# A decoder trunk on one core: the feed-forward output projection as seven half-size products

## The chip, the cores and the metric

The kernel runs on one core of a Trainium2 chip. The metric is the device time in microseconds (us) of one execution; the time before is the median of three runs. A core has TensorE (PE, matrix products, with its weight loads shown as PEld), VectorE (DVE), ScalarE (ACT), GpSimd (POOL) and SyncE (SP), each with an instruction queue of its own that is worked off in order, and 16 DMA engines that all queues share. SP, ACT and POOL issue transfers.

## The reference, cut to what matters

Two layers, each with a mixer (layer 0: forgetting attention beside a short convolution; layer 1: a gated linear recurrence), a cross-attention into 256 memory rows, and a feed-forward block; 512 positions, width 1024, all fp32. The change is in the feed-forward block's second product:

```python
D_MODEL = 1024; SEQ = 512; DEPTH = 2
D_FF = ((8 * D_MODEL // 3 + 255) // 256) * 256        # 2816

def rmsnorm(x, g):
    y = x * lax.rsqrt(jnp.mean(x * x, axis=-1, keepdims=True) + EPS)
    return y * g

def swiglu(h, w_gu, w_down):
    g, u = jnp.split(h @ w_gu, 2, axis=-1)
    return (jax.nn.silu(g) * u) @ w_down

    # in each layer, after the mixer and the cross-attention:
    h = rmsnorm(x, g_ffn_pre[layer])
    y = swiglu(h, w_ffn_gu[layer], w_ffn_down[layer])
    x = x + rmsnorm(y, g_ffn_post[layer])
```

## The kernel before

**Precision.** Every fp32 operand is split in two: a high part (an ACT cast to fp32r) and a low part (a DVE subtraction). A product is three matmuls: high x high, high x low, low x high (`mm3` L298, `OutProj.mm` L530). `split_out` (L506) does one split; for weights it has [128, 1024] elements.

**Order.** PE's order is written by hand in the whole kernel (`manual_schedule(engines={PE})`, L49). In the feed-forward stream ACT, DVE and POOL follow the program's order too (L868); elsewhere a scheduler orders them. SP is always ordered by the scheduler.

**Buffers.** `gpool` has 14 groups of [128, 4, 512]; `wst` four staging buffers for raw weights (tag `st`); `whi` and `wlo` four buffers each for their high and low parts; two PSUM pools, `bankA` and `bankB`, four banks of [128, 512] each.

**Stages of a layer.** Mixer, its output projection (`OutProj`, in two sweeps: `half0` for output columns 0 to 511, `half1` for 512 to 1023), memory projections (`memory_kv` L671), queries, scores and output projection of the cross-attention (`cross` L704), feed-forward (`ffn` L794). The feed-forward input product already runs as seven half-size products per chunk of 256 columns (`Winograd.stream` L443): 20 chunks, each of seven products of 12 matmuls with 256 columns, 84 in all; the first two column chunks are made before by `ws_gemm_split` (L354). Its activations y (22 k-tiles of 128 rows, 512 positions) go to DRAM by `put_y` (L806) and come back by `load_y` (L839), both on POOL's queue.

**The output projection before the change.** `pf` (L1272) is an `OutProj` with 22 k-tiles. `half0` (L563) loads the weights of two k-tiles at a time ([128, 2, 512], 512 KB), splits them, and multiplies them with all four tiles of 128 positions: 22 x 4 x 3 matmuls of 512 columns. `half1` (L570) does the same for the other columns, and leaves the last eight k-tiles (`TAIL`) for the end, one position tile after the other, so that the tail of one tile (`chain` L594: square sum, root, gain, residual; `next` L610: the next layer's pre-norm; `transpose` L617) lies beside the matmuls of the next tile. The root is `rstd` (L200): two small DVE operations and a power on POOL. In layer 0 the last two position tiles are transposed from `hook` (L620), which the next layer's `ws_gemm_split` calls between its first blocks of 24 matmuls; in layer 1 the rows go to the output.

Of the kernel before, what the change touches and what calls it, by code (L numbers as in the profile page):

```python
# [25 lines left out]
LEAD = 2  # L26
# [16 lines left out]
def trunk_kernel(ctx: ExitStack, tc: tile.TileContext, a: dict, out: bass.AP):  # L43
# [83 lines left out]
    def load_rows(w, k0, n, c0):  # L127
# [5 lines left out]
        return hi, lo  # L133

# [219 lines left out]
    def ws_gemm_split(w, c0s, hT, hook):  # L354

        wss = [w_chunk(w, c0) for c0 in c0s]
        banks = [[bankA() for _ in range(2)] for _ in c0s]
# [15 lines left out]
    class Winograd:  # L373
# [30 lines left out]
        def load(self, w, c0):  # L404
# [3 lines left out]
            for kh in range(2):  # L408
                nc.sync.dma_start(out=r[kh], in_=rows[:, 4 * kh:4 * kh + 4, c0:c0 + 256])
# [108 lines left out]
    class OutProj:  # L518
        def __init__(self, w, y, nk, g_post, g_pre, hT, first=bankA, second=bankB, final=False):
# [6 lines left out]
            self.ready = {}  # L526
            self.ahead = self.gate = None
# [10 lines left out]
        def half0_steps(self, ks, first, last):  # L538
# [5 lines left out]
            for n, k in enumerate(ks):  # L544
                wt = self.ready.pop(k) if k in self.ready else load_w(self.w, k, 2, 0, 512)
                if self.ahead:
                    for k2 in ks[n + LEAD:n + LEAD + 1]:
                        self.ahead(k2)
# [76 lines left out]

        def run(self):
            self.half0(range(0, self.nk, 2), True, True)
            self.half1()
# [165 lines left out]
    def ffn(layer, hT, prev, proj):  # L794
        w = a["w_ffn_gu"][layer]
        y = Feat([None] * NFF, [None] * NFF)

        y2 = dram.tile([P, NFF, 512], F32, name=f"y2_{layer}")
        yraw, yback = {}, {}

        def y_rows(jp):

            yraw[jp] = wst.tile([P, 2, 512], F32, tag="st", name="yr")
            return yraw[jp]

        def put_y(jp):  # L806
            nc.gpsimd.dma_start(out=y2[:, 2 * jp:2 * jp + 2, :], in_=yraw[jp])

        def act(jp, s, ub):
            y_ = y_rows(jp)  # L810
            for m in range(2):
                nc.vector.tensor_tensor(out=y_[:, m, :], in0=s[m], in1=ub[m], op=ALU.mult)
            put_y(jp)

        def chunks(jp):
# [10 lines left out]
            def up(m, sl, ps, sb, op):  # L826
                if not y_:
                    y_.append(y_rows(jp))
                ym = y_[0][:, m, :]
                nc.vector.tensor_tensor(out=ym[:, sl], in0=ps, in1=sb, op=op)  # L830
                mult = lambda: nc.vector.tensor_tensor(out=ym, in0=ym, in1=s[m], op=ALU.mult)
                if m == 1:
                    mult()
                    put_y(jp)
# [4 lines left out]
        def load_y(i):  # L839
            n = min(4, NFF - 4 * i)  # L840
            yback[i] = f(group("yb"))
            nc.gpsimd.dma_start(out=yback[i][:, 0:n, :], in_=y2[:, 4 * i:4 * i + n, :])

        def parts(jp):
            if jp // 2 not in yback:
                load_y(jp // 2)
            yg = group("y")
            split_out(yback[jp // 2][:, jp % 2 * 2:jp % 2 * 2 + 2, :], yg[:, 0:2, :], yg[:, 2:4, :])
            for m in range(2):
                y.hi[2 * jp + m], y.lo[2 * jp + m] = yg[:, m, :], yg[:, 2 + m, :]  # L850

        def side(left):

            if left == 3:
                load_y(0)
            if left:
                return {}
            raw = [load_raw(proj.w, k, 2, 0, 512) for k in (0, 2)]
            for i in (1, 2):
                load_y(i)  # L860

            def weights(n):
                proj.ready[2 * n] = split_w(raw[n], 2, 512)

            return {"a": lambda: weights(0), "b": lambda: parts(0), "c": lambda: weights(1), "d": lambda: parts(1)}

        gb, ub = ws_gemm_split(w, [0, FF], hT, prev.hook)
# [5 lines left out]
        proj.y = y  # L873
# [426 lines left out]
```

## Time and profile before

| | us |
|---|---|
| median of three runs (lowest, highest) | 1419.03 (1418.71, 1419.05) |
| the profiled execution | 1419.26 |
| its span, first to last instruction | 1417.5 |
| layer 0's output projection of the feed-forward | 622.6 to 744.1 |
| layer 1's | 1291.2 to 1411.0 |

Times of single steps are read from the profiled execution, counted from the start of its span; that execution lasted 1.8 us longer than its span. A row of a group ("lines") gives line, engine, operation, tiles and shapes, count, busy time and mean duration, and the idle time before it with what ended it. A row of the timeline gives start, duration, engine, line, operation. A row of windows gives, for a stretch, the busy time of PE, PEld, DVE, ACT and POOL (instructions), the granted clock of PE as a share of full speed, the share of the 16 DMA engines, and GB/s. A row of DMA issues ends with the median time from issue to landing. PE's instructions overlap, so the distance between their starts, not their duration, is what one costs.

### The profile page before, as it was taken

The page shows a single profiled execution, that of the slowest core. Times are in us where ns is not written, and L with a number is a line of the kernel's source. Part 1 is how long each engine was busy: PE and PEld are TensorE (multiplying, and loading weights), DVE is VectorE, ACT ScalarE, POOL GpSimd, SP SyncE. Part 2 cuts the span into 40 slices and gives each one's busy share as a digit, 9 for nine tenths or more (in the row PEclk, how much of TensorE's full clock was granted, in tenths as well). Part 3 has the DMA queues.
Part 4 walks back from the last instruction along what each step waited for, and adds up shares of the span by engine and source line. Part 5 has one row for each costly group of instructions (what it writes and reads, how often), then busy time and mean ns, then how long its engine had stood idle before and what let it go on. Part 6 is the DMA issues. An engine that isn't in the chain of part 4 may idle for free.

```text
span 1417.5 us, 21486 instructions
## 1 busy us (share of the span) xinstructions
PE 1406.5 (99%) x8564; PEld 1252.3 (88%) x8564; DVE 1013.9 (72%) x1623; ACT 663.6 (47%) x1069; POOL 55.9 (4%) x116
## 2 busy tenths in 40 slices
PE   8999999999999999999999999999999999999998
PEld 6778789888899999998889888988889999999886
DVE  5776777635689999992447898754478999998232
ACT  4354455433565444452334896543356444445130
POOL 1000001000000000010000000100000000000000
PEclk9999999999999999999999999999999999999999
DMA  5633152521234434373512336252023334347321
GB/s 175 190 89 99 56 184 83 194 90 45 68 117 144 148 121 138 131 266 120 164 52 82 104 93 198 97 178 89 31 80 114 129 125 147 122 144 272 104 74 60
DMA packets 124287, 174.34 MB, mean 123 GB/s; under 512 B 6725, under 2 KB 88721, under 8 KB 122906
## 3 DMA queue, kind: packets, MB, share of 16 engines
q1 hardware_dynamic: 114722, 140.92, 31.3%
q0 software_dynamic: 5568, 25.18, 4.8%
q10 hardware_dynamic: 3896, 6.86, 1.6%
q8 instruction: 67, 1.10, 0.3%
q14 instruction: 34, 0.28, 0.1%
HBM read 159.29 MB, written 13.65 MB: 122 GB/s over the span
## 4 chain that ended last, share of the span: by engine, by line
PE 99%; DMA 1%; ACT 0%; DVE 0%; DVEq 0%; POOLq 0%; issue 0%; SPq 0%; ACTq 0%
PE bA L299 14%; PE bA L301 14%; PE bA L300 14%; PE bB L300 6%; PE bB L299 6%; PE bB L301 6%; PE bA L534 5%; PE bA L536 5%; PE bA L535 5%; PE bB L535 5%; PE bB L534 5%; PE bB L536 5%; PE bA L905 2%; PE bB L283 1%; PE bA L697 1%; PE bA L699 1%
## 5 line engine op out<-in xcount | busy, mean ns | idle before, releaser
L510 DVE TENSOR_TENSOR wl<-st,wh 128x1024 fp32r<-128x1024 f32 x148 | 180.5, 1223 | 187.8 <-ACT wh L509 186.6
L509 ACT CAST wh<-st 128x1024 fp32r<-128x1024 f32 x148 | 155.3, 1051 | 214.4 <-PE bA L300 66.1
L299 PE MATMUL bA<-hTh,wh 128*128 128x512 f32 (+1 forms) x448 | 171.4, 383 | 0.0
L301 PE MATMUL bA<-hTh,wl 128*128 128x512 f32 (+1 forms) x448 | 168.0, 375 | 0.0
L300 PE MATMUL bA<-hTl,wh 128*128 128x512 f32 (+1 forms) x448 | 167.7, 374 | 0.0
L401 ACT CAST wg<-wr 128x1024 fp32r<-128x1024 f32 x80 | 83.6, 1046 | 49.1 <-DVE wr L430 37.6
L301 PEld LDWEIGHTS bA<-hTh,wl 128*128 128x128 f32 x448 | 84.3, 188 | 15.4
L402 DVE TENSOR_TENSOR wg<-wr,wg 128x1024 fp32r<-128x1024 f32 x80 | 97.4, 1217 | 0.0
L300 PEld LDWEIGHTS bA<-hTl,wh 128*128 128x128 f32 x448 | 84.5, 189 | 13.6
L299 PEld LDWEIGHTS bA<-hTh,wh 128*128 128x128 f32 x448 | 84.5, 189 | 13.5
L534 PE MATMUL bB<-wh,y 128*128 128x512 f32 x208 | 80.9, 389 | 0.0
L535 PE MATMUL bB<-wl,y 128*128 128x512 f32 x208 | 80.9, 389 | 0.0
L536 PE MATMUL bB<-wh,y 128*128 128x512 f32 x208 | 80.9, 389 | 0.0
L401 ACT CAST wh<-tt 128x1024 fp32r<-128x1024 f32 x40 | 42.1, 1052 | 61.2 <-DVE tt L430 61.2
L299 PE MATMUL bA<-hTq,wh 128*128 128x256 f32 x208 | 59.2, 284 | 0.0
L301 PE MATMUL bA<-hTq,wl 128*128 128x256 f32 x208 | 58.9, 283 | 0.0
L300 PE MATMUL bA<-hTq,wh 128*128 128x256 f32 x208 | 58.9, 283 | 0.0
L534 PE MATMUL bA<-wh,y 128*128 128x512 f32 x144 | 56.5, 392 | 0.0
L536 PE MATMUL bA<-wh,y 128*128 128x512 f32 x144 | 56.1, 390 | 0.0
L535 PE MATMUL bA<-wl,y 128*128 128x512 f32 x144 | 56.1, 389 | 0.0
L402 DVE TENSOR_TENSOR wl<-tt,wh 128x1024 fp32r<-128x1024 f32 x40 | 48.7, 1219 | 0.0
L534 PEld LDWEIGHTS bB<-wh,y 128*128 128x128 f32 x208 | 39.1, 188 | 8.1
(330 smaller groups left out, 4171.7 us busy)
## 6 DMA issues: line engine op xcount, KB each, us to landing
wr<-in_w_ffn_gu_dram SPq DMA_DIRECT2D x80, 512.0 KB, 4.6
st<-in_w_ffn_down_dram SPq DMA_DIRECT2D x44, 512.0 KB, 3.9
st<-in_w_xkv_dram SPq DMA_DIRECT2D x32, 512.0 KB, 4.6
st<-in_ab_w_in_dram SPq DMA_DIRECT2D x24, 512.0 KB, 3.8
y<-yr POOLq DMA_DIRECT2D x22, 512.0 KB, 3.9
yb<-y POOLq DMA_DIRECT2D x10, 1024.0 KB, 7.0
st<-in_w_xq_dram SPq DMA_DIRECT2D x16, 512.0 KB, 3.4
st<-in_w_xo_dram SPq DMA_DIRECT2D x16, 512.0 KB, 3.9
```

The costliest lines, as they stand in the source:

```text
L283: nc.tensor.transpose(out=ps[:, j * P:(j + 1) * P], in_=hs[hf][:, j * P:(j + 1) * P], identity=ident)
L299: nc.tensor.matmul(out=ps, lhsT=wh, rhs=xh, start=first, stop=False)
L300: nc.tensor.matmul(out=ps, lhsT=wh, rhs=xl, start=False, stop=False)
L301: nc.tensor.matmul(out=ps, lhsT=wl, rhs=xh, start=False, stop=last)
L401: return (lambda: nc.scalar.copy(out=to[0], in_=src), lambda: nc.vector.tensor_tensor(out=to[1], in0=src, in1=f(to[0]), op=ALU.subtract))
L402: lambda: nc.vector.tensor_tensor(out=to[1], in0=src, in1=f(to[0]), op=ALU.subtract))
L509: nc.scalar.copy(out=hi, in_=src)
L510: nc.vector.tensor_tensor(out=lo, in0=src, in1=f(hi), op=ALU.subtract)
L534: nc.tensor.matmul(out=ps, lhsT=yh, rhs=wh[:, kk, :], start=first, stop=False)
L535: nc.tensor.matmul(out=ps, lhsT=yh, rhs=wl[:, kk, :], start=False, stop=False)
L536: nc.tensor.matmul(out=ps, lhsT=yl, rhs=wh[:, kk, :], start=False, stop=last)
L905: nc.tensor.matmul(out=banks[t], lhsT=(hT.lo if c == "x" else hT.hi)[k][:, ts], rhs=(wl if c == "w" else wh)[:, kk, :], start=passes[t] == ...
```

## The change

The output projection y (512 x 2816) times W (2816 x 1024) is cut in half in all three sizes: positions in two halves, k-tiles into even and odd, output columns in two halves. Instead of eight half-size products it makes seven, one after the other, from sums and differences of the quarters (`ORDER`): each is 11 k-tiles x 2 position tiles x 3 matmuls of 512 columns. The operands on the activation side (`n3`, `s2`, `n1`, `n4`) are differences made by DVE in place in SBUF, where all of y is held in six groups. Those on the weight side (`t1` to `t4`) are sums in DRAM, made ahead of time by transfers: a copy of one quarter on SP's queue, then an adding transfer on POOL's queue. There are 20 such pairs for each layer (five slices of k-tiles x four sums, 512 or 768 KB each). `pace` issues them: with every fourth weight load (`EVERY`), counted from the first layer's mixer on, it issues the adds of the copies before, and one more copy behind that load.

Products go in 42 items of two k-tiles (one in each sixth); 12 matmuls make an item. `run` writes out the order of ACT, DVE and POOL around them by items (`at[g]` is issued ahead of item g): low parts of weights two items ahead, casts three ahead, activations five and six ahead, and the reading of the products' banks, gains, roots, row updates, pre-norm at set items of products 5 to 7. The last product's last four items (`KEPT`) are done first for position tile 2 and then for tile 3; between the two lie, in layer 0, the casts of the next layer's first weights (`hi_f`) and the transposes of position tiles 0 and 1. Tiles 2 and 3 are transposed from `hook` as before. `ws_gemm_split` takes weights that are already split, and its order in layer 1 is written too.

```diff
+EVERY = 4
-        nc.sync.dma_start(
+        pace(nc.sync.dma_start(
             out=st, in_=w.rearrange("(k p) n -> p k n", p=P)[:, k0:k0 + nk, c0:c0 + c]
-        )
+        ))
+    def pace(load):
+        loads[0] += 1
+        if loads[0] > 0 and loads[0] % EVERY == 0:
+            for add in later[:]:
+                add()
+                later.remove(add)
+            if todo:
+                copy, add = todo.pop(0)
+                with tc.issue_after(load.ins):
+                    copy()
+                later.append(add)
...
-    def ws_gemm_split(w, c0s, hT, hook):
-        wss = [w_chunk(w, c0) for c0 in c0s]
+    def ws_gemm_split(wss, hT, hook):
...
+    class DownProj(OutProj):
+        NJ = NFF // 2
+        NG = (NFF + 3) // 4
+        ORDER = (("a11", "b11"), ("a22", "t4"), ("n3", "t3"), ("s2", "t2"), ("n1", "t1"), ("a12", "b21"), ("n4", "b22"))
+        SUMS = {"n3": ("a21", "a11"), "s2": ("a22", "n3"), "n1": ("a11", "s2"), "n4": ("a12", "s2")}
+        GROUPS = 0, 1, 2, 4, 3, 5
+        KEPT = 4
+        def plan(self):
+            for js in ((0, 2), (2, 4), (4, 6), (6, 8), (8, self.NJ)):
+                for to, frm, add in (("t3", "b12", "b22"), ("t2", "b11", "t3"), ("t4", "b21", "t2"), ("t1", "b11", "b12")):
+                    todo.append((
+                        lambda to=to, frm=frm, js=js: nc.sync.dma_start(out=self.rows(to, *js), in_=self.rows(frm, *js)),
+                        lambda to=to, add=add, js=js: nc.gpsimd.dma_start(
+                            out=self.rows(to, *js), in_=self.rows(add, *js), accum_op=ALU.add),
+                    ))
...
+        def hi_b(self, s):
+            if s >= len(self.items):
+                return
+            self.load_b(s)
...
+            if keep >= 0:
+                if keep % 2 == 0:
+                    self.kept = group("rh"), group("rl")
+                self.wt[s] = [g[:, keep % 2 * 2:keep % 2 * 2 + n, :] for g in self.kept]
+            else:
+                self.wt[s] = [pool.tile([P, n, 512], F32R, tag=tag, name=tag) for pool, tag in ((whi, "wh"), (wlo, "wl"))]
+            nc.scalar.copy(out=self.wt[s][0], in_=self.st[s])
...
+        def hi_f(self, n):
...
+            st = load_raw(w, 4 * kh, 4, c0s[c], 256)
+            hi = whi.tile([P, 4, 256], F32R, tag="wh", name="wh")
+            lo = wlo.tile([P, 4, 256], F32R, tag="wl", name="wl")
...
+            nc.scalar.copy(out=hi, in_=st)
...
+        def run(self):
...
+            made = 3
+            for g in range(M):
+                n = 2 if g < 2 else 1
+                for u in range(made, min(made + n, M)):
+                    do(g, lambda u=u: self.lo_a(u), lambda u=u: u + 1 < M and self.hi_a(u + 1))
+                    if u + 2 < M and self.items[u + 2][0][0] != "n4":
+                        do(g, lambda u=u: self.sub(u + 2))
+                made = min(made + n, M)
+                do(g, lambda g=g: g + 2 < M - KEPT + 1 and self.lo_b(g + 2), lambda g=g: g + 3 < M - KEPT + 1 and self.hi_b(g + 3))
+            for n, g in enumerate((23, 27, 28, 29, 31, 32)):
+                do(g, lambda n=n: self.sub(6 * N + n))
+            for n, (g, h) in enumerate(((36, 36), (36, 37), (37, 37))):
+                do(g, lambda n=n: self.hi_b(M - 3 + n))
+                do(h, lambda n=n: self.lo_b(M - 3 + n))
+            do(N, lambda: [nc.scalar.copy(out=p1[t], in_=bk[0][t]) for t in range(2)])
+            do(4 * N, lambda: [tt(q[t], bk[3][t], p1[t], ALU.subtract) for t in range(2)])
+            do(4 * N + 1, lambda: [tt(v[t], bk[2][t], q[t], ALU.add) for t in range(2)])
+            do(4 * N + 2, lambda: [tt(c21[t], bk[1][t], v[t], ALU.subtract) for t in range(2)])
+            do(4 * N + 3, lambda: [self.square(t, 0, c21[t]) for t in range(2)])
+            do(4 * N + 4, lambda: [self.gain(0, c21[t]) for t in range(2)])
+            for t in range(2):
+                do(5 * N + t, lambda t=t: tt(v[t], bk[4][t], v[t], ALU.add), lambda t=t: self.square(t, 1, v[t]))
+            for t in range(2):
+                do(5 * N + 1 + t, lambda t=t: self.gain(1, v[t]))
+                do(5 * N + 2 + t, lambda t=t: self.add(t, (c21[t], v[t])))
+                do(5 * N + 3 + t, lambda t=t: tt(q[t], bk[4][t], q[t], ALU.add))
+                if not self.final:
+                    do(5 * N + 3 + t, lambda t=t: self.pre(t))
+                    do(5 * N + 4 + t, lambda t=t: self.scale(t))
+            do(6 * N, lambda: [(tt(p1[t], bk[5][t], p1[t], ALU.add), self.square(2 + t, 0, p1[t])) for t in range(2)])
+            do(6 * N + 1, lambda: [self.gain(0, p1[t]) for t in range(2)])
...
+            late = range(M - KEPT, M)
+            for s in late:
+                self.mms(s, (0,), bk[6])
+            if not self.final:
+                for n in range(4):
+                    self.hi_f(n)
+                self.transpose(0)
+                self.lo_f(0)
+                self.transpose(1)
+                self.lo_f(1)
+            end = lambda t: (tt(q[t], bk[6][t], q[t], ALU.add), self.square(2 + t, 1, q[t]), self.gain(1, q[t]))
+            end(0)
+            self.add(2, (p1[0], q[0]))
+            if not self.final:
+                self.pre(2)
+                self.lo_f(2)
+                self.lo_f(3)
+            for s in late:
+                self.mms(s, (1,), bk[6])
+            end(1)
+            if not self.final:
+                self.scale(2)
+            self.add(3, (p1[1], q[1]))
+        def hook(self, m):
+            if m == HOOKS[0]:
+                self.transpose(2)
+                self.next(NT - 1)
+            elif m == HOOKS[1]:
+                self.transpose(3)
...
         def side(left):
-            if left == 3:
-                load_y(0)
+            if left == 1:
+                proj.load_y(0)
             if left:
                 return {}
...
+            for i in (1, 2, 4, 3):
+                proj.load_y(i)
+            return {"a": lambda: (proj.hi_b(0), proj.hi_a(0), proj.hi_b(1), proj.lo_b(0), proj.lo_a(0)),
+                    "c": lambda: (proj.hi_a(1), proj.hi_b(2), proj.lo_b(1), proj.lo_a(1)),
+                    "d": lambda: (proj.hi_a(2), proj.lo_a(2), proj.hi_a(3))}
...
-        b0, b1 = ws_gemm_split(w, [D, D + 256], hT, prev.hook)
+        with tc.manual_schedule(engines={mybir.EngineType.Activation, mybir.EngineType.DVE, mybir.EngineType.Pool}):
+            b0, b1 = ws_gemm_split(prev.follow, hT, prev.hook)
```

In this diff `lo_a`/`hi_a` and `lo_b`/`hi_b` are the low and high parts of the activations' and the weights' operand of an item, `sub` the difference for one, `mms` its matmuls; `square` is ACT's sum of squares, `gain` a multiplication by the post-norm's gain, `add` the root and the update of a tile's rows of x, `pre` and `scale` the next pre-norm's statistics and its scaling. N is 6 items to a product, M is 42.

More of the change, by code (lines that the diff above doesn't have):

```diff
@@ L25 @@
 TAIL = 8
-LEAD = 2
+EVERY = 4
 HOOKS = 0, 2
@@ L133, in load_rows @@
         return hi, lo
+    todo, later = [], []
+    loads = [-1 << 30]
+    def pace(load):
[9 more added lines that the diff above has]
+                later.append(add)
     vectors = (
@@ L352, in weave @@
             advance()
-    def ws_gemm_split(w, c0s, hT, hook):
-        wss = [w_chunk(w, c0) for c0 in c0s]
-        banks = [[bankA() for _ in range(2)] for _ in c0s]
+    def ws_gemm_split(wss, hT, hook):
+        banks = [[bankA() for _ in range(2)] for _ in wss]
         for half in range(2):
@@ L408, in load @@
             for kh in range(2):
-                nc.sync.dma_start(out=r[kh], in_=rows[:, 4 * kh:4 * kh + 4, c0:c0 + 256])
+                pace(nc.sync.dma_start(out=r[kh], in_=rows[:, 4 * kh:4 * kh + 4, c0:c0 + 256]))
             return r
@@ L525, in __init__ @@
             self.tails = {}
-            self.ready = {}
-            self.ahead = self.gate = None
+            self.gate = None
             self.hs = [None] * NT
@@ L543, in half0_steps @@
                 self.banks = [self.first() for _ in range(NT)]
[L544 to L548, printed above, removed]
+            for k in ks:
+                wt = load_w(self.w, k, 2, 0, 512)
                 for kk in range(2):
@@ L795, in ffn, with pair @@
         w = a["w_ffn_gu"][layer]
[L796 to L807, printed above, removed]
         def act(jp, s, ub):
-            y_ = y_rows(jp)
+            ym = proj.y_rows(jp)
             for m in range(2):
-                nc.vector.tensor_tensor(out=y_[:, m, :], in0=s[m], in1=ub[m], op=ALU.mult)
-            put_y(jp)
+                nc.vector.tensor_tensor(out=ym[m], in0=pair(s[m]), in1=pair(ub[m]), op=ALU.mult)
+            proj.put_y(jp)
+        def pair(ap):
+            return ap.rearrange("p (h c) -> p h c", c=256)
         def chunks(jp):
@@ L832, in up @@
                 if m == 1:
                     mult()
-                    put_y(jp)
+                    proj.put_y(jp)
                 return mult if sl.start == 0 else None
             return [(w, jp * 256, bankB, gate), (w, FF + jp * 256, bankA, up)]
[L839 to L850, printed above, removed]
@@ L872, in ffn @@
                                 {"act0": silu(0), "act1": silu(1)}, lambda: act(0, first, ub), side)
-        proj.y = y
-        proj.ahead = lambda k: parts(k // 2)
-        proj.run()
+            proj.run()
     def fox(proj):
@@ L974, in fox @@
                 mm_v(k0, 3)
+        loads[0] = 0
         setup_chan()
@@ L1271, in trunk_kernel @@
         hT = new_hT() if layer == 0 else None
-        pf = OutProj(a["w_ffn_down"][layer], None, NFF, a["g_ffn_post"][layer],
-                     a["g_mix_pre"][1], hT, first=bankB, second=bankA, final=layer == 1)
+        pf.hT = hT
         ffn(layer, hTf, pc, pf)
```

154 lines of the change are left out of this document (141 added, 13 removed).

## The prediction

> **What bounds the kernel now.** I read the page from the top: busy times, the chain that ended last, then who waited for whom on TensorE.
>
> ```profile
> span 1417.5 us, 21486 instructions
> PE 1406.5 (99%) x8564; PEld 1252.3 (88%) x8564; DVE 1013.9 (72%) x1623; ACT 663.6 (47%) x1069; POOL 55.9 (4%) x116
> PE 99%; DMA 1%; ACT 0%; DVE 0%; DVEq 0%; POOLq 0%; issue 0%; SPq 0%; ACTq 0%
> PE bB L283 <- DVE h L236: 1.6, 2, 1.2
> PE bA L905 <- ACT hTh L292: 1.5, 1, 1.5
> PE bB L892 <- POOL ident masks.py:199: 1.5, 1, 1.5
> ```
>
> TensorE runs without a break: three waits of 1.5 us or so, all in the first 12 us. So every matmul taken away is worth its spacing, until another engine takes the lead. Next, the stage that changes, layer 0's down projection: its first and last matmul, its repeated matmul, its busy times.
>
> ```profile
> 622.59 0.40 PE L534 MATMUL bB<-wh,y 128*128 128x512 f32 x1
> 743.87 0.39 PE L536 MATMUL bA<-rh,y 128*128 128x512 f32 x1
> L534 PE MATMUL bB<-wh,y x86: 389/389/389, 624.0 to 681.8; 128*128 128x512 f32 x86
> 622.50:744.20 121.70, 121.70 (x548) 100.95 (x547) 56.07 (x70) 40.60 (x59) 4.73 (x9) 1.00 0.41 137
> ```
>
> Matmuls overlap, so a duration of 389 ns isn't their cost. L534 is each third one: its 86 rows span 85 x 3 spacings, 57.8 / 255 = 0.2267 us. The stage has 22 x 4 x 2 x 3 = 528 of them, 119.7 us, and 16 transposes; 622.6 to 744.1 is 121.5. The window row (after the seconds: PE, PEld, DVE, ACT, POOL busy, clock, DMA share, GB/s) says what is free: DVE works 56 of 122 us, ACT 41.
>
> **TensorE's share.** Seven products of 11 k-tiles x 2 token tiles x 3 are 462 matmuls of the same shape, 66 fewer: 66 x 0.2267 = 15.0 us a layer, **-29.9 us** in both. A product takes 66 x 0.2267 = 15.0 us, an item (two k-tiles, 12 matmuls) 2.72.
>
> **VectorE.** Its price by size is the distance between starts where it runs without a break, not the duration:
>
> ```profile
> 597.21 1.22 DVE L402 TENSOR_TENSOR wg<-wr,wg 128x1024 fp32r<-128x1024 f32 x1
> 598.34 0.69 DVE L430 TENSOR_TENSOR tt<-t,wr 128x512 f32<-128x512 f32 x1
> 598.95 0.42 DVE L449 TENSOR_TENSOR wy<-bA,wx 128x256 f32<-128x256 f32 x1
> 599.28 0.68 DVE L402 TENSOR_TENSOR wl<-t,wh 128x512 fp32r<-128x512 f32 x1
> ...
> 614.45 1.05 ACT L509 CAST wh<-st 128x1024 fp32r<-128x1024 f32 x1
> 615.40 1.05 ACT L509 CAST y<-yb 128x1024 fp32r<-128x1024 f32 x1
> ...
> 726.90 0.16 DVE L206 SCALAR_TENSOR_TENSOR post<-post 128x1 f32<-128x1 f32 x1 [3.85 <-ACT junk L198]
> 727.80 0.75 DVE L602 SCALAR_TENSOR_TENSOR x<-ya,post,x 128x512 f32<-128x512 f32 x1
> 728.47 0.75 DVE L602 SCALAR_TENSOR_TENSOR x<-yb,post,x 128x512 f32<-128x512 f32 x1
> 728.65 0.63 ACT L198 ACTIVATE junk<-x 128x512 bf16<-128x512 f32 x1 [1.78 <-DVE x L602]
> 729.40 0.63 ACT L198 ACTIVATE junk<-x 128x512 bf16<-128x512 f32 x1
> ```
>
> So 1024 columns cost 1.13, 512 cost 0.60, 256 cost 0.33, a row update 0.67, a root (DVE, POOL and back) 0.85 if nothing stands between, an ACT cast 0.95, a square 0.75. Each product now needs its weight low parts (5 x 1.13 + 0.6 = 6.3), activation low parts (5 x 0.6 + 0.33 = 3.3) and in four products differences (3.3): 12.9 of 15.0 us. ACT casts 5.3 + 3.0 = 8.3. In products 1 to 4 TensorE thus stays the bound, but DVE can't save up work: the four wh and wl buffers hold it to about three items ahead.
>
> From the end of product 4 (4 x 15.0 = 59.9, counted from the stage's first matmul) the written order adds the reading of sums, gains, roots and row updates. Layer 0, DVE in its order: the split of item 26 waits for the buffer of item 22, so DVE begins with q at 61.1. Up to the weight split of item 36 it has eight splits of 1024 (9.0), 28 operations of 512 (16.8), two of 256 (0.7), four row updates (2.7), three small statistics (0.4), and waits for POOL (1.8): 31.4, done at 92.5. TensorE wants it at 6 x 15.0 = 89.8: **2.8 late**. Behind it, two scalings, a q, a split and a weight split make item 37 1.1 late, and the same kind of queue item 40 0.7 late: 4.6 in all. The three items of cover are used up by then; without them it would be 8 more.
>
> **Layer 0's end.** After the late products of token tile 2 (at 105.7) TensorE transposes tiles 0 and 1. ACT has four casts of the next layer's weights (hi_f) queued ahead of the copies that empty these banks. The fourth needs a staging buffer that DVE's split of item 41 frees at about 104, its load goes behind the third's (104.7), and lands so much later:
>
> ```profile
> st<-in_w_ffn_down_dram SPq DMA_DIRECT2D x44, 512.0 KB, 3.9
> st<-in_w_xkv_dram SPq DMA_DIRECT2D x32, 512.0 KB, 4.6
> ```
>
> 108.7, cast to 109.7, first bank copied 110.2 and split 110.9; with the handovers the bank is free for tile 1 at 111.4: **5.7 us** of TensorE, where a bare evacuation (0.53 + 0.6 and handovers) would cost 1.2.
>
> Then a chain: from 110.7 DVE has four bank splits, four weight splits, the ends of both tiles, the root, row update and pre-norm of tile 2 (with ACT's two squares) and its scaling: 14.4 us by the prices above, 125.1. TensorE meanwhile has the rest of tile 1's transposes, the late products of tile 3 (21 x 0.2267 = 4.8) and the next layer's first 24 matmuls before the hook asks for tile 2. Their price:
>
> ```profile
> 395.67 0.28 PE L299 MATMUL bA<-hTq,wh 128*128 128x256 f32 x1
> 398.54 1.18 PE L283 MATMUL bB<-ident,h 128*128 128x128 f32 x8
> ```
>
> 24 in 2.87. TensorE is there at 120.0, so it waits **5.2 us**. Before, tiles 0 and 1 came in the middle of the last sweeps, and there was no wait here.
>
> Such pauses can cost more than themselves. The granted clock (third figure from the end of a window row) around the kernel's first pauses:
>
> ```profile
> 9.08 0.66 PE L283 MATMUL bB<-ident,h 128*128 128x128 f32 x4 [1.23 <-DVE h L236]
> 11.21 1.22 PE L905 MATMUL bA<-wh,hTh 128*128 128x512 f32 x2 [1.47 <-ACT hTh L292]
> 12.22 1.05 PE L905 MATMUL bA<-wl,hTh 128*128 128x512 f32 x2
> 8.00:12.00 4.00, 1.45 (x6) 0.94 (x7) 2.05 (x3) 2.02 (x3) 0.00 (x0) 0.73 1.04 409
> 12.00:16.00 4.00, 4.00 (x10) 3.19 (x10) 3.29 (x8) 2.60 (x4) 1.47 (x1) 0.50 1.03 366
> 16.00:20.00 4.00, 4.00 (x20) 2.92 (x19) 2.66 (x5) 2.30 (x6) 0.00 (x0) 0.92 0.55 158
> ```
>
> The clock lost there is 4 x (0.27 + 0.50 + 0.08) = 3.4 us, after pauses of only 1.2 and 1.5 us. Three pauses in layer 0 (2.8, 5.7, 5.2) cost between 0 and 3 x 3.4; I take one, **3.4**, since those first pauses fell in a stretch where TensorE worked 1.5 of 4 us, and here it works fully around them. [...]
>
> **Layer 1.** No pre-norm and scaling: the split of item 36 comes 0.6 earlier, **2.2 late**, later ones in time. At the end:
>
> ```profile
> 1410.72 0.39 PE L536 MATMUL bA<-rh,y 128*128 128x512 f32 x1
> 1411.20 0.60 ACT L198 ACTIVATE junk<-bA 128x512 bf16<-128x512 f32 x1 [4.75 <-PE bA L536]
> 1413.48 0.75 DVE L602 SCALAR_TENSOR_TENSOR x<-yb,post,x 128x512 f32<-128x512 f32 x1
> ```
>
> The last sum must first be added to q (0.6 and a handover) before its square: **+0.9**.
>
> **Transfers.** A product now reads 2.9 MB of weights in 15 us, 193 GB/s, over twice the old pace. Of a staging buffer's cycle (four buffers, 4 x 2.5 = 10 us on average) one item (2.5) and a split (1.13) are taken, so a load may land 6.3 us after its issue; rows above say 3.9 to 4.6. Cost taken: nothing. The added copies and adds (40 of each, one per four loads, 0.5 or 0.75 MB) meet the densest loads in the memory projections:
>
> ```profile
> 245.00:255.00 10.00, 10.00 (x86) 10.00 (x85) 6.11 (x6) 4.49 (x6) 0.00 (x0) 1.00 0.69 227
> 265.00:275.00 10.00, 10.00 (x46) 8.29 (x45) 6.18 (x6) 4.91 (x6) 0.00 (x0) 1.00 0.59 184
> ```
>
> No adding transfer is in the trace. If an add costs as much as a load, the share rises from 0.59 to 0.59 x 1.5 = 0.89, hidden; if it costs three (two reads, one write), to 1.18, and 45 us of that stage would stretch by some 8 us a layer, less what the eight buffers hide. I take nothing, the nearer row, and keep 0 to 7 a layer. An add also waits on POOL's queue for its copy, with the roots (0.56 each) behind it; it is queued four loads after the copy, 4 x 2.72 = 10.9 us at the fastest, so the copy has landed. The sums are complete at load 84 of 105, ten chunks before use.
>
> **Sum** against the profiled execution, 1419.3 us (its span is 1417.5; the median 1419.03 is the same within 0.02%): 1419.3 - 29.9 + 4.6 + 5.7 + 5.2 + 3.4 + 2.2 + 0.9 = **1411.4 us**.
>
> **Rivals.**
> - DVE keeps up. If the waits for POOL and ACT in its order are shorter than counted, item 41's split comes before TensorE's late products, no item is late, the transposes cost 1.2 and the hook perhaps 2: 1419.3 - 29.9 + 1.2 + 2 + 0.9 = 1393.5, band 1390 to 1404. For: ACT has 6 us of slack a product; against: 31.4 us of DVE work stands against 28.7 of TensorE whoever waits. Chance 0.26.
> - Adds cost stretch in the memory projections, about 3.5 a layer: 1418, within 0.2%. For: share 0.69 before any of it; against: eight buffers of cover. Chance 0.14.
> - **Slower**: loads in the down projection land later than 6.3 us, since 193 GB/s now meet y's return at the start. Each us over costs 42 / 4 = 10.5 a layer; the forecast's 8 us of gain are gone at 6.7 us, and at 7 the time is 1411.4 + 14.7 = 1426. For: packets of 2 KB, and the memory projections' median is 4.6 already; against: these move 227 GB/s at that. Chance 0.14.
> - The forecast, DVE late at the end: band 1404 to 1416. Chance 0.46.
>
> Measurement tells about 0.2% (2.8 us) from no change. Faster: 0.46 + 0.26 = 0.72; within: 0.14; slower: 0.14. The range 1394 to 1424 leaves out about 0.06 below and 0.11 above.
>
> **What would show it.** Matmuls with 512 columns at 0.227 us, 462 to a layer; DVE busy over nine tenths of layer 0's last two products; waits of TensorE on wl near item 36, on the first bank's split at the second transposes, on h at the next layer's hook, each followed or not by a clock under 1; DMA from issue to landing under 6 us. Wrong it would be if TensorE waits on weight casts all along the stage (landing), or in the memory projections (adds), or nowhere (DVE keeps up).

## The result and the profile after

The changed kernel takes 1425.78 us (median of five runs, 1424.48 to 1426.60) against 1419.05 (1418.71 to 1419.43): a ratio of 1.0047, 95% interval [1.0032, 1.0061]. It is slower, by 6.7 us; the forecast was 1411.4, in a range that ended at 1424. The profiled execution of the changed kernel lasted 1424.48 us.

The page of the changed kernel: its span, the busy times, the chain that ended last.

```profile
span 1422.7 us, 21768 instructions
PE 1386.5 (97%) x8432; PEld 1232.6 (87%) x8432; DVE 1116.3 (78%) x1801; ACT 720.0 (51%) x1175; POOL 109.3 (8%) x154
PE 86%; DVE 7%; DMA 3%; ACT 2%; issue 2%; POOL 1%; SPq 0%; DVEq 0%; POOLq 0%; ACTq 0%
```

TensorE has the 132 matmuls less that the change promises (8564 to 8432). The chain was 99% TensorE; now it is 86%. Who it waits for, in its waits (us in total, times, longest):

```profile
PE bB L940 <- DVE mem L925: 8.8, 1, 8.8
PE bB L300 <- DVE hTl L310: 5.5, 1, 5.5
PE bB L791 <- DVE wl L761: 5.3, 2, 2.9
PE bB L300 <- DVE h L253: 5.0, 3, 3.8
```

Three of the four were in the forecast: the late weight splits (`wl`), the first bank at the second transposes (`hTl`), the hook's transposes (`h`). The longest was not: it lies in the memory rows, some 150 us behind the changed stage. The same waits in TensorE's timeline, in brackets at the end of each row:

```profile
714.93 0.50 PE L791 MATMUL bB<-wl,ya 128*128 128x512 f32 x1 [2.92 <-DVE wl L761]
733.71 1.97 PE L300 MATMUL bB<-ident,h 128*128 128x128 f32 x8 [5.54 <-DVE hTl L310]
748.95 1.65 PE L300 MATMUL bB<-ident,h 128*128 128x128 f32 x8 [3.79 <-DVE h L253]
895.90 1.97 PE L940 MATMUL bB<-ident,mem 128*128 128x128 f32 x8 [8.84 <-DVE mem L925]
1398.55 0.80 PE L791 MATMUL bB<-wl,ya 128*128 128x512 f32 x1 [2.36 <-DVE wl L761]
```

And windows around them (PE, PEld, DVE, ACT, POOL busy; then clock, DMA share, GB/s):

```profile
712.00:718.00 6.00, 3.08 (x10) 2.40 (x10) 5.89 (x11) 3.63 (x7) 0.73 (x1) 0.80 0.34 111
718.00:724.00 6.00, 6.00 (x26) 4.94 (x25) 6.00 (x9) 1.56 (x2) 0.14 (x1) 0.92 0.34 108
...
730.00:736.00 6.00, 2.29 (x10) 2.20 (x11) 2.94 (x4) 3.76 (x6) 0.00 (x0) 0.72 0.13 48
736.00:742.00 6.00, 6.00 (x21) 4.79 (x20) 4.29 (x9) 1.02 (x3) 0.55 (x1) 0.71 0.53 176
...
748.00:754.00 6.00, 5.02 (x29) 4.84 (x30) 4.53 (x11) 2.62 (x6) 1.90 (x5) 0.72 0.65 213
...
892.00:898.00 6.00, 2.10 (x9) 2.10 (x10) 2.07 (x5) 0.69 (x2) 2.29 (x3) 0.50 0.49 76
...
1398.00:1404.00 6.00, 5.45 (x18) 4.37 (x19) 6.00 (x9) 0.64 (x2) 0.00 (x0) 0.72 0.59 191
```

DVE is full (5.89 and 6.00 of 6 us) in the two windows around the first late split; during or behind each of these waits the clock falls.

Where the 5.2 us between the two spans come from, by the starts of the same matmuls in both traces:

| stretch | before | after | difference |
|---|---|---|---|
| layer 0's down projection, from its first matmul to the next stage's | 121.5 | 120.3 | -1.2 |
| from there to the memory rows' transposes in layer 1 | 139.0 | 153.8 | +14.8 |
| from there to the memory key projection | 19.9 | 21.9 | +2.0 |
| from there to layer 1's down projection | 388.2 | 388.2 | 0.0 |
| layer 1's down projection, first matmul to last | 119.5 | 108.6 | -10.9 |
| from the last matmul to the end | 6.8 | 8.1 | +1.3 |

These add up to 6.0; the work ahead of the first stretch is 0.8 shorter. The second stretch holds the hook (5.8 of the 14.8) and the memory rows (9.0; with the 2.0 behind it, 11.0).

**The memory rows' wait.** The memory rows are normalized like any others: two small DVE operations, a power on POOL (the root), a scaling, then the transposes. DVE's timeline before the change:

```profile
881.07 0.16 DVE L206 SCALAR_TENSOR_TENSOR mem<-mem 128x1 f32<-128x1 f32 x1
881.96 1.42 DVE L646 SCALAR_TENSOR_TENSOR mem<-mem,gain 128x512 f32<-128x512 f32 x2 [0.73 <-POOL mem L210]
```

DVE's timeline after it:

```profile
884.85 0.16 DVE L223 SCALAR_TENSOR_TENSOR mem<-mem 128x1 f32<-128x1 f32 x1
895.09 1.41 DVE L925 SCALAR_TENSOR_TENSOR mem<-mem,gain 128x512 f32<-128x512 f32 x2 [10.09 <-POOL mem L227]
```

The root took 0.73 us; now it takes 10.09. POOL's timeline of the changed kernel says why:

```profile
865.19 1.14 POOL L676 DMA_DIRECT2D t<-in_w_ffn_down_dram  x1 [22.20 <-DMA t<-in_w_ffn_down_dram]
879.93 1.14 POOL L676 DMA_DIRECT2D t<-t  x1 [13.60 <-DMA t<-in_w_ffn_down_dram]
893.32 1.14 POOL L676 DMA_DIRECT2D t<-t  x1 [12.25 <-DMA t<-in_w_ffn_down_dram]
894.03 1.02 POOL L227 TENSOR_TENSOR mem<-mem,nhalf 128x1 f32<-128x1 f32 x1
```

The copies stand in SP's timeline:

```profile
872.18 0.56 SPq L675 DMA_DIRECT2D t<-in_w_ffn_down_dram  x1
...
880.95 0.56 SPq L675 DMA_DIRECT2D t<-in_w_ffn_down_dram  x1
```

Three adds stand ahead of the root in POOL's queue, each waiting for its copy. The root's operand is there at 885.0; POOL has been standing at the third add since 881, and that add's copy, issued at 880.95, releases it only at 893.3, over 12 us later. The root goes at 894.03, and TensorE, which had nothing else in its order, has waited 8.84 us. Over the whole kernel POOL waits so at 29 of its adds (POOL's waits):

```profile
POOL t L676 <- DMA t<-in_w_ffn_down_dram: 543.4, 29, 40.6
```

Almost everywhere that costs nothing, because nothing is wanted from POOL meanwhile.

### The profile page after: what moved, and what is told of

Read it like the earlier page. It is cut to its first block, busy times and chain, and to the rows that moved or that the text cites. A ratio compares the mean times of both kernels' runs of the same rounds, so it can differ in the third digit from the quotient of the medians.

```text
span 1422.7 us, 21768 instructions
## 1 busy us (share of the span) xinstructions
PE 1386.5 (97%) x8432; PEld 1232.6 (87%) x8432; DVE 1116.3 (78%) x1801; ACT 720.0 (51%) x1175; POOL 109.3 (8%) x154
## 4 chain that ended last, share of the span: by engine, by line
PE 86%; DVE 7%; DMA 3%; ACT 2%; issue 2%; POOL 1%; SPq 0%; DVEq 0%; POOLq 0%; ACTq 0%
PE bA L316 13%; PE bA L318 13%; PE bA L317 13%; PE bB L316 6%; PE bB L317 6%; PE bB L318 6%; PE bB L791 2%; PE bA L549 2%; PE bB L792 2%; PE bA L550 2%; PE bB L790 2%; PE bA L551 2%; DVE wl L761 1%; PE bB L551 1%; PE bB L549 1%
## 5 line engine op out<-in xcount | busy, mean ns | idle before, releaser
L526 DVE TENSOR_TENSOR wl<-st,wh 128x1024 fp32r<-128x1024 f32 x108 | 131.5, 1222 | 99.4 <-ACT wh L525 98.3
L525 ACT CAST wh<-st 128x1024 fp32r<-128x1024 f32 x108 | 113.3, 1050 | 123.4 <-PE bA L317 70.7
L756 ACT CAST wh<-st 128x1024 fp32r<-128x1024 f32 x76 | 74.8, 984 | 57.6 <-issue 35.6
L318 PEld LDWEIGHTS bA<-hTh,wl 128*128 128x128 f32 x448 | 84.9, 189 | 15.5
L761 DVE TENSOR_TENSOR wl<-st,wh 128x1024 fp32r<-128x1024 f32 x76 | 86.2, 1135 | 13.4 <-ACT wh L756 13.4
L791 PE MATMUL bB<-wl,ya 128*128 128x512 f32 x148 | 59.3, 400 | 5.3 <-DVE wl L761 5.3
L790 PE MATMUL bB<-wh,ya 128*128 128x512 f32 x148 | 58.7, 397 | 0.0
L792 PE MATMUL bB<-wh,ya 128*128 128x512 f32 x148 | 58.6, 396 | 0.0
L736 DVE TENSOR_TENSOR ya<-yb,ya 128x512 fp32r<-128x512 f32 x84 | 53.3, 639 | 0.0
L790 PE MATMUL bA<-wh,ya 128*128 128x512 f32 x132 | 51.3, 389 | 0.0
L791 PE MATMUL bA<-wl,ya 128*128 128x512 f32 x132 | 51.3, 389 | 0.0
```

What stands on the lines that cost most here:

```text
L318: nc.tensor.matmul(out=ps, lhsT=wl, rhs=xh, start=False, stop=last)
L525: nc.scalar.copy(out=hi, in_=src)
L526: nc.vector.tensor_tensor(out=lo, in0=src, in1=f(hi), op=ALU.subtract)
L756: nc.scalar.copy(out=self.wt[s][0], in_=self.st[s])
L761: nc.vector.tensor_tensor(out=lo, in0=self.st[s], in1=f(hi), op=ALU.subtract)
L790: nc.tensor.matmul(out=banks[t], lhsT=yh, rhs=wh[:, jj, :], start=first and jj == 0, stop=False)
```

## The experiments

My theory from this profile: (1) the order of adds and roots on POOL costs 11 us in the memory rows; (2) what was forecast at the end of layer 0 and in DVE's fullness is there and costs what was forecast. The rivals: the adds' traffic itself delays the memory rows (then the order would change little); the hook and the transposes are held by TensorE's own order or by ACT; the clock, not the waits, makes the rest.

### First round: one cause at a time, each on the changed kernel

**e1_order** issues every add behind the last root that the program has written so far; nothing else changes.

```diff
+    roots = [None]
...
             for add in later[:]:
-                add()
+                with tc.issue_after(roots[0].ins):
+                    add()
...
-        nc.gpsimd.tensor_tensor(out=st[:, 4:5], in0=st[:, 3:4], in1=nhalf, op=ALU.pow)
+        roots[0] = nc.gpsimd.tensor_tensor(out=st[:, 4:5], in0=st[:, 3:4], in1=nhalf, op=ALU.pow)
```

> The same work; on POOL's queue each adding transfer now stands behind the last root that was traced before it, so no root waits behind an add whose copy is still under way. Theory (layer 1's memory rows waited 8.8 us for a root that stood behind an add, and TensorE ran 2 us longer at a lower clock after it): 1425.8 - 11 = 1414.8 us, with TensorE's wait before the memory transposes gone and layer 0's down projection as it was. Rival (the memory rows came late because copies and adds crowd the 16 DMA engines there): the traffic is the same, so the wait stays and the time is 1425 within 2 us.

**e2_noadd** takes the adds away and keeps the copies.

```diff
             for add in later[:]:
-                add()
                 later.remove(add)
```

> All adding transfers are left out, so the weight sums hold one quarter only; the copies stay. Theory of the queue: the same 11 us as with the adds reordered, 1414.8 us, since the adds' bytes cost nothing by themselves. Rival of the traffic: the wait shrinks only as far as the adds' share of the traffic goes, and every stage with dense loads gets a little shorter, 1418 to 1422 us.

**e3_tfirst** puts three of the four casts of the next layer's weights behind the transposes of tiles 0 and 1.

```diff
-                for n in range(4):
-                    self.hi_f(n)
+                self.hi_f(0)
                 self.transpose(0)
-                self.lo_f(0)
                 self.transpose(1)
+                for n in range(1, 4):
+                    self.hi_f(n)
+                self.lo_f(0)
                 self.lo_f(1)
```

> The same work; at the end of layer 0's down projection three of the four casts of the next layer's weights stand behind the transposes of tiles 0 and 1 on ScalarE's queue, no longer ahead of their copies. Theory (the 5.5 us wait for the first bank is ScalarE's queue waiting for weight loads): the wait falls to about 1.2 us, and about 1.5 us of lower clock goes with it, 1425.8 - 5.8 = 1420 us. Rival (VectorE is behind there anyway, so the bank's low part comes late whatever stands ahead on ScalarE): no change, 1425.8 us within 1.5.

**e4_chain** moves two weight splits (`lo_f` 2 and 3) and the last gain behind the scaling of tile 2, which the hook's first transposes want.

```diff
                 self.pre(2)
-                self.lo_f(2)
-                self.lo_f(3)
...
-            end(1)
+            tt(q[1], bk[6][1], q[1], ALU.add)
+            self.square(3, 1, q[1])
             if not self.final:
                 self.scale(2)
+                self.lo_f(2)
+                self.lo_f(3)
+            self.gain(1, q[1])
```

> The same work; on VectorE's queue at the end of layer 0's down projection the scaling of tile 2 stands ahead of two weight splits of the next layer and of the last gain. Theory (the hook's transposes wait 3.8 us because VectorE's queue reaches that scaling last): the wait falls below 1 us, about 1 us of clock goes with it, but tile 3's transposes now wait about 2 us, since its own chain isn't shorter: 1425.8 - 3 = 1422.8 us. Rival (the wait is for the root or for ScalarE's squares): no change within 1 us. In layer 1 only the last gain moves, at no cost.

Measured, against the kernel before on the same chip (its median 1418.52; in the four measurements of this document it lies between 1418.51 and 1419.05, so differences between rounds hold to about 0.5 us):

| kernel | median (lowest, highest) | ratio to before [95%] |
|---|---|---|
| e1_order | 1414.34 (1413.43, 1415.46) | 0.9969 [0.9958, 0.9981] |
| e2_noadd | 1414.46 (1413.09, 1415.71) | 0.9970 [0.9958, 0.9981] |
| e3_tfirst | 1420.24 (1417.28, 1423.06) | 1.0012 [1.0003, 1.0021] |
| e4_chain | 1423.24 (1417.68, 1424.73) | 1.0024 [1.0012, 1.0036] |

The order alone takes 11.4 us off 1425.78. POOL's timeline of e1_order in the memory rows of layer 1:

```profile
886.99 0.56 POOL L229 TENSOR_TENSOR mem<-mem,nhalf 128x1 f32<-128x1 f32 x1 [61.28 <-DVE mem L225]
889.49 0.55 POOL L229 TENSOR_TENSOR mem<-mem,nhalf 128x1 f32<-128x1 f32 x1 [1.93 <-DVE mem L225]
889.99 1.16 POOL L678 DMA_DIRECT2D t<-in_w_ffn_down_dram  x1
```

POOL is free when the root's operand comes, and the add follows behind both roots. The wait of TensorE on `mem` is gone; the two at layer 0's end are still there (5.70 us for the first bank, 5.16 at the hook). Taking the adds away altogether gives the same time to 0.1 us: the adds' own traffic has no price that these runs can see; it was their place in the queue. So the rival that puts it down to traffic falls.

TensorE's waits in e3_tfirst (the profiled execution is the longest of its ten, 1423.06):

```profile
PE bB L300 <- DVE h L253: 9.8, 4, 6.7
...
PE bB L300 <- DVE hTl L310: 1.0, 1, 1.0
```

The first bank's wait falls from 5.5 to 1.0, so the casts in front of it were its cause; the hook's grows from 3.8 to 6.7, so part of the gain is given back at the next stop. In all 5.5 us between the medians. In e4_chain the hook's two waits are 1.38 us for tile 2 and 1.73 for tile 3, where the changed kernel waits 3.79 for tile 2 alone; but its profiled execution (1418.64) also had a shorter wait on `mem` (6.4), and its runs spread over 7 us, so the 2.5 us between the medians can't all be put down to the edit. The spread of e3 and e4, 6 and 7 us where the changed kernel has 2, goes with the granted clock: e3's four executions of up to 1419.40 us had a mean clock of 0.992 and the six others 0.988 or 0.989; e4's three under 1419 had 0.992 or 0.993, the others 0.987 to 0.992. The last section has a possible reason.

### Second round: the rest, on top of e1_order

**f1_end** writes layer 0's end anew: one weight cast ahead of the transposes, the root of tile 2 issued between the two, its row update, pre-norm and scaling ahead of the late products of tile 3, the other casts and splits around them. `add` is cut for this into `root` and `update`.

```diff
+                self.hi_f(0)
+                tt(q[0], bk[6][0], q[0], ALU.add)
+                self.transpose(0)
+                self.square(2, 1, q[0])
+                self.gain(1, q[0])
+                self.root(2)
+                self.transpose(1)
+                self.update(2, (p1[0], q[0]))
+                self.hi_f(1)
+                self.lo_f(0)
+                self.pre(2)
+                self.lo_f(1)
+                self.scale(2)
                 for s in late:
                     self.mms(s, (1,), bk[6])
+                tt(q[1], bk[6][1], q[1], ALU.add)
+                self.square(3, 1, q[1])
+                self.hi_f(2)
+                self.lo_f(2)
+                self.gain(1, q[1])
+                self.root(3)
+                self.hi_f(3)
+                self.lo_f(3)
+                self.update(3, (p1[1], q[1]))
```

> The reordered queue of POOL, and the end of layer 0's down projection in another order, with the same work: one cast ahead of the transposes instead of four, tile 2's sum read before them, its root, row update and pre-norm between the weight splits so that VectorE doesn't stand while ScalarE and POOL work, its scaling ahead of tile 3's end. Theory (both waits there are an engine's queue order, and the clock falls only because of them): by the prices of the prediction VectorE reaches tile 2's scaling 1.5 us before TensorE asks, the waits of 5.7 and 5.2 us go, and 2 to 3 us of lower clock with them: 1414.3 - 12 = 1402 us. Rival (VectorE has too much work there in any order): the wait moves to tile 3's transposes or to the next layer's weights, 1408 to 1412 us.

**f2_relief** takes load from DVE's fullest stretch in both layers: the six differences for the last product stand at items 18 to 21, 29 and 32 in place of 23 to 32, and each row update, with the pre-norm and scaling behind it, stands one item later than its root, so that DVE doesn't stand waiting for POOL.

```diff
-            for n, g in enumerate((23, 27, 28, 29, 31, 32)):
+            for n, g in enumerate((18, 19, 20, 21, 29, 32)):
...
-                do(5 * N + 2 + t, lambda t=t: self.add(t, (c21[t], v[t])))
+                do(5 * N + 2 + t, lambda t=t: self.root(t))
+                do(5 * N + 3 + t, lambda t=t: self.update(t, (c21[t], v[t])))
...
-                    do(5 * N + 3 + t, lambda t=t: self.pre(t))
-                    do(5 * N + 4 + t, lambda t=t: self.scale(t))
+                    do(5 * N + 4 + t, lambda t=t: self.pre(t))
+                    do(5 * N + 5 + t, lambda t=t: self.scale(t))
```

> The reordered queue of POOL, and in products 4 to 6 the same work in another order: three of the last product's differences one product earlier, and each root issued an item before its row update, so that VectorE doesn't stand. Theory (item 36 is 2.9 and 2.4 us late because VectorE has 31.4 us of work against 28.7 of TensorE): 1.8 us of work and 1.7 us of standing less, so the wait before item 36 falls to about 0 in both layers and some 1.5 us of lower clock with each: 1414.3 - 7 = 1407 us, less if the later wait for the first bank takes back layer 0's part (1410). Rival (the weights' loads or casts are late there): no change, 1414 us.

**f3_both** is both edits.

> All three changes of order together. If they are independent: 1414.3 - 12 - 7 = 1395 us, with no wait of TensorE over 1 us after the first 20 us of the kernel, and 1419 - 30 + 2 = 1391 as the floor that the removed matmuls set.

| kernel (before: 1418.93) | median (lowest, highest) | ratio to before [95%] |
|---|---|---|
| f1_end | 1405.68 (1404.51, 1406.89) | 0.9907 [0.9893, 0.9922] |
| f2_relief | 1405.73 (1405.42, 1406.03) | 0.9908 [0.9891, 0.9925] |
| f3_both | 1398.63 (1398.48, 1399.07) | 0.9858 [0.9844, 0.9873] |

Each edit takes 8.6 or 8.7 us off e1_order, and the two together 15.7. f1_end stayed 3.7 above its expectation and f3_both 3.6, with waits of 3.0 and 1.8 us where none over 1 was expected; f2_relief came out 1.3 below its 1407. What is left of TensorE's waits in f3_both:

```profile
PE bB L302 <- DVE h L255: 4.7, 4, 3.0
...
PE bB L793 <- DVE rl L763: 1.8, 1, 1.8
...
PE bA L320 <- DVE wl L780: 0.8, 1, 0.8
PE bB L302 <- DVE hTl L312: 0.4, 1, 0.4
```

The first bank (0.4) and the weight splits at item 36 (none) are settled; 1.8 us are left at item 40's (`rl`). With f2's edit alone layer 1's down projection takes 104.5 us, 119.5 less exactly the 15.0 of its 66 matmuls. The hook's wait of 3.0 is the largest left, with the 0.8 just ahead of it.

### Third round: the hook's rest, and whether the causes are independent

DVE's timeline of f3_both just ahead of that wait shows it idle, for a cast that ACT has queued behind the last square sum:

```profile
734.44 0.69 DVE L829 TENSOR_TENSOR c<-bB,c 128x512 f32<-128x512 f32 x1
736.91 1.23 DVE L780 TENSOR_TENSOR wl<-st,wh 128x1024 fp32r<-128x1024 f32 x1 [1.79 <-ACT wh L776]
```

**g1_casts** is f3_both with both casts ahead of that square.

```diff
+                self.hi_f(2)
+                self.hi_f(3)
                 self.scale(2)
...
                 self.square(3, 1, q[1])
-                self.hi_f(2)
                 self.lo_f(2)
...
-                self.hi_f(3)
                 self.lo_f(3)
```

> Everything of f3_both, and ACT's third and fourth cast of the next layer's weights stand ahead of the last square sum instead of behind it. In f3_both ACT stands idle from 731 to 735.2, then makes the square and the two casts back to back, and DVE waits 1.79 us for the first cast; gain, root, row update, pre-norm and scaling of position tile 3 come behind it, and TensorE waits 3.0 us for h and 0.8 for the fourth wl, with a clock below 1 for some 10 us after it (about 1.7 us). If that chain is what is left of the stage's loss, tile 3 is ready some 2.4 us earlier and the wait falls under 1 us: 1398.6 - 2.4 - 0.8 - (0 to 1.7) = 1393.7 to 1395.4. Rival: the chain is held by its own steps (square, root on POOL, update, squares, root, scaling), not by the casts: 1398.6 within 1 us. Should the clock keep its loss although the wait is under 1 us, the cause of the clock isn't the length of the wait.

**g2_noorder** is f3_both without e1's order.

> f3_both without the order of adding transfers behind the roots: the new end of layer 0 and the earlier differences and roots alone. If the two causes are independent, the memory rows' root again waits on POOL for a copy, and the time is 1398.6 + 11.4 (what the order alone took off the changed kernel, 1425.8 to 1414.3) = 1410.0. Rival: the waiting of the adds depends on when the copies and adds happen to be issued and land, and what stands ahead of the root changes with every shift of some us: then it may be anywhere from 1398.6 (no add in front of the root) to 1412.

| kernel (before: 1418.51) | median (lowest, highest) | ratio to before [95%] |
|---|---|---|
| g1_casts | 1396.50 (1395.59, 1398.10) | 0.9845 [0.9830, 0.9859] |
| g2_noorder | 1409.36 (1408.78, 1412.21) | 0.9940 [0.9924, 0.9957] |

g2_noorder: 10.7 us above f3_both, where e1_order stood 11.4 below the changed kernel. That is what two independent causes give, and the root again stands behind the adds in POOL's timeline:

```profile
870.97 1.14 POOL L676 DMA_DIRECT2D t<-t  x1 [14.81 <-DMA t<-in_w_ffn_down_dram]
881.70 1.14 POOL L676 DMA_DIRECT2D t<-t  x1 [9.60 <-DMA t<-t]
882.42 1.02 POOL L227 TENSOR_TENSOR mem<-mem,nhalf 128x1 f32<-128x1 f32 x1
```

The last add waits 9.60 us here, for the add before it (`t<-t`) and not for its copy as expected. The price isn't fixed: TensorE waits 7.4 us on `mem` here, 8.8 in the changed kernel, 8.6 in e3_tfirst and 6.4 in e4_chain.

g1_casts came out 2.1 us below f3_both, short of the 3.2 to 4.9 expected. The 0.8 on the fourth `wl` is gone, but of the hook's 3.0 us 2.2 are left (TensorE's timeline):

```profile
743.30 1.23 PE L302 MATMUL bB<-ident,h 128*128 128x128 f32 x8 [2.16 <-DVE h L255]
```

Tile 3 came 1.8 us earlier, as its chain should; but without the wait on `wl`, TensorE also stood at the transposes 1.0 earlier (741.1 for 742.1). By DVE's timeline, and not tested further, what holds it now is the chain's own length (sum, square, root, row update, squares, root, scaling, from 734.5 to 743.3); the casts were only part of it. So neither the theory (wait under 1 us) nor its rival (no change) came true as it stood. Of all versions g1_casts is the fastest: 22.0 us under the kernel before, 29.3 under the changed one.

## Why the prediction was wrong, by its steps

**TensorE's share**: right. Nothing else in the way, layer 1's stage loses exactly the 15.0 us (104.5 in f2_relief), and g1's sum closes: 1419.3 - 29.9 = 1389.4; with g1's waits, all around layer 0's end (2.2 + 1.8 + 0.4), 1.7 of clock and 1.3 at the tail it comes to 1396.8, measured 1396.5.

**VectorE, late items**: right in place and size. Item 36 was to be 2.8 late in layer 0 and 2.2 in layer 1; it was 2.92 and 2.36. Items 37 and 40 were to cost 1.1 and 0.7 more; in the changed kernel they cost 0 and 0.2, because TensorE ran at a lower clock behind the first wait and DVE caught up. In e4_chain, whose edit lies behind these items, the clock stayed at 1.00 there, and they cost 0.96 and 0.47 (TensorE's timeline, items 36, 37 and 40):

```profile
716.13 0.50 PE L791 MATMUL bB<-wl,ya 128*128 128x512 f32 x1 [2.93 <-DVE wl L761]
720.12 0.50 PE L791 MATMUL bB<-wl,ya 128*128 128x512 f32 x1 [0.96 <-DVE wl L761]
726.38 0.50 PE L791 MATMUL bB<-rl,ya 128*128 128x512 f32 x1 [0.47 <-DVE rl L761]
```

**Layer 0's end**: right in mechanism. The first bank was to cost 5.7 and cost 5.54, from the casts ahead of it (e3_tfirst shows it). From the stage's first matmul TensorE stood there from 106.3 to 111.9, where the forecast has 105.7 to 111.4; its 105.7 is the end of tile 0's transposes (441 x 0.2267 + 4.6 + 1.1), though the text names the late products. The hook was to cost 5.2 and cost 3.79: the scaled tile came at 127.1 instead of 125.1, and TensorE, slowed by the clock, at 123.3 instead of 120.0. In e1_order TensorE came at 122.1 and waited 5.16.

**The clock**: mis-sized. One charge of 3.4 was taken for layer 0. By the windows quoted, (1 - clock) x 6 us gives 1.2 + 0.5 behind item 36, 1.7 + 1.7 around the first bank, 1.7 at the hook: 6.8, twice the charge. The stage's own account agrees: of the 13.8 us by which it missed its gain of 15.0, the waits (2.9, 0.2, 5.5) are 8.7, which leaves 5.1 for the clock. Layer 1's 2.36 us brought another 1.7, for which nothing was taken. Together the stage and the hook lost 13.8 + 5.8 = 19.6 us of layer 0's gain, where the forecast's terms are 18.9. That this total is close is in part luck: the waits are 12.5 for a forecast of 15.5, the clock 6.8 for 3.4. The two are linked here: TensorE, at a clock of 0.50 behind the first bank's wait, came 3.3 us later to the hook than forecast (123.3 for 120.0), and its wait there was 1.4 us shorter (3.79 for 5.2).

**The tail**: 1.3 for 0.9.

**Transfers, the step that failed.** The adds' traffic was costed at nothing, and e2_noadd (0.1 us from e1_order) bears that out. But the text goes on: "An add also waits on POOL's queue for its copy, with the roots (0.56 each) behind it; it is queued four loads after the copy, 4 x 2.72 = 10.9 us at the fastest, so the copy has landed." The mechanism is named there and dismissed by a time that isn't one. First, "four loads after" is a place in the program. POOL has nothing of the loads in its queue that would hold an add back: as soon as one add is issued it stands at the next and waits there, which is what the 29 waits in POOL's list (543.4 us) say. Second, 2.72 us is the pace of the down projection; outside it loads come at the scheduler's own pace: the two copies quoted lie 8.8 us apart, and the second released its add 12.4 us after its own issue. Third, POOL's order outside the written stretch is the scheduler's, and it put adds ahead of the memory rows' root. The step should have asked, root by root, what stands ahead of it on POOL; then it would have had a rival of one root's wait, up to a copy's issue distance and landing, and the slower side would have come from there and not from late loads. 11.4 us (e1_order) is more than the whole forecast gain of 7.9; with that one term the forecast would have been 1411.4 + 11.4 = 1422.8, against 1425.8.

Of the remaining 3.0 us, layer 1's clock (1.7), the stage and the hook (0.7) and the tail (0.4) are 2.8.

**The rivals.** "DVE keeps up" (1393.5) is what f2, f3 and g1 approach by hand: 1396.5. "Adds cost stretch in the memory projections" did not happen: the stretch from the memory key projection to layer 1's down projection is 388.2 us in both, and the work ahead of layer 0's down projection is 0.8 us shorter. "Loads land later than 6.3 us" did not happen in the down projection, by the median (the last figure) of the changed kernel's DMA issues:

```profile
st<-t SPq DMA_DIRECT2D x40, 512.0 KB, 3.8
t<-in_w_ffn_down_dram SPq DMA_DIRECT2D x32, 512.0 KB, 5.5
st<-in_w_ffn_down_dram SPq DMA_DIRECT2D x30, 512.0 KB, 3.3
...
t<-in_w_ffn_down_dram POOLq DMA_DIRECT2D x16, 512.0 KB, 7.6
t<-t POOLq DMA_DIRECT2D x16, 512.0 KB, 8.3
```

## What to carry to other kernels

An add that stood 12.25 us at its copy on POOL's queue held up the root behind it here, and the time fell by 11.4 us when the adds were put behind the roots. So before a transfer that waits for another one is added, list for each small operation on its engine (a root, a statistic) what will stand ahead of it, and tie the transfer behind the operation if the order isn't written out. Four loads behind the copy was a place in the program and no time: check what the queue itself has to wait for before "it has landed by then" is used as a reason. When TensorE is the bound and gets less work, go through the full stretches of the next engine and what can be moved ahead of them: here that was worth 15.7 us (e1_order to f3_both), more than half of what the removed matmuls themselves were.

## What the runs showed of the hardware that was not expected

**In these runs clock was lost in steps of 1.7 us, and waits of one size cost different numbers of them.** In the traces of the kernel before and of the changed kernel the clock is 1.00 or 0.50, and up to the last matmul a spell at 0.50 lasts 3.41 us, or two or three times that (6.83 in the kernel before; 3.41, 6.83, 3.41, 10.24 and 3.41 in the changed one); 3.41 us at half the clock are 1.7 us lost. In the changed kernel the spells start at 715.60, 732.66, 749.73, 889.68 and 1398.26, and the last four are 5, 10, 51 and 200 times 3.41 us behind the first. Windows cut in stretches of 3.41 us from those starts (the second figure is PE's busy time) in the changed kernel:

```profile
712.19:715.60 3.41, 0.67 (x3) 0.58 (x4) 3.41 (x6) 2.81 (x7) 0.00 (x0) 1.00 0.05 18
715.60:719.01 3.41, 3.41 (x10) 2.63 (x9) 3.30 (x7) 1.48 (x2) 0.86 (x1) 0.50 0.49 154
```

The same in e4_chain:

```profile
714.34:717.75 3.41, 1.62 (x7) 1.37 (x8) 3.41 (x5) 3.07 (x7) 0.00 (x0) 1.00 0.16 44
717.75:721.17 3.42, 2.46 (x12) 1.68 (x11) 3.31 (x7) 1.05 (x1) 0.86 (x1) 1.00 0.32 116
```

And in g1_casts, at the hook:

```profile
741.43:744.85 3.42, 1.55 (x13) 1.40 (x14) 1.84 (x4) 0.99 (x4) 0.97 (x10) 1.00 0.62 227
744.85:748.26 3.41, 3.41 (x19) 3.41 (x18) 1.03 (x2) 0.30 (x1) 1.21 (x1) 0.50 0.73 162
```

Item 36 of layer 0 waits the same 2.9 us in both of the first two. In the changed kernel 2.74 us of it lie in one stretch, and the next stretch runs at half the clock. In e4_chain 1.79 us of it lie in the first stretch quoted and 1.14 ahead of it, and both stretches quoted run at the full clock. In f1_end the same wait, 2.93 us up to 714.70, is followed by matmuls 0.43 us apart until 720.42, where they are 0.23 apart before 711.4 and again from 720.7: about two stretches, 3.4 us lost. Layer 1's wait (2.36 us in the changed kernel, 2.35 in e4_chain, 2.36 in f1_end) cost none in the last two: the matmuls behind it are 0.23 apart, and layer 1's down projection takes 107.2 us there, and 108.6 in the changed kernel.

In the changed kernel's trace, from 20 us to the last matmul, five such stretches at full clock have TensorE idle for 2.07 to 3.41 us (2.74, 3.41, 2.66, 2.62 and 2.07), and each is followed by one at half clock; no other stretch at full clock there has over 1.16 us. Of those at half clock, the ones with 1.04, 3.41 and 2.81 us idle are followed by another at half clock, those with 0.00 and 0.29 by full clock. The rows of g1_casts above add a stretch at full clock with 1.87 us idle, from the hook's single gap of 2.16, that is followed by half clock, and those of e4_chain one with 1.79 that isn't. In the kernel before, one with 1.69, from 6.42 us of its span, is. So these traces give no one length up to which a wait is free of cost; the ends of matmuls are modelled, so the idle times are rough. If the place of the stretches differs between executions of one kernel, that would explain the spread of e3 and e4; it isn't shown, since only one execution of each has a trace.

**An add took two to two and a half times a down-projection load's time from issue to landing in the changed kernel** (medians of 7.6 and 8.3 us for 512 KB, rows above, against 3.3 and 3.8 for a load into SBUF and 5.5 for a plain copy), without a price in the kernel's time that e2_noadd could show (0.1 us from e1_order).
